# Modulation rows stored through a transpose, and two row tiles scaled at another place, in a one-layer diffusion backbone

## The chip, the cores and the metric

The kernel runs on one core of a Trainium2 chip. The metric is the device time of one execution in microseconds (us); below it is given as the median of three runs, and the profile comes from one further execution.

Names used here: PE is TensorE (matrix products), PEld its weight loads, ACT is ScalarE, DVE is VectorE, POOL is GpSimd, SP is SyncE, which issues most transfers (SPq in the profile). All work is float32. A product is made from three matmuls, since each operand is split into a high part and a low remainder: high by high, high by low, low by high.

## The reference

One layer, for 1024 latent tokens and 128 context tokens, width 1024. A conditioning vector gives six modulation vectors; the third (`ga1`) and the sixth (`ga2`) scale the two residual branches. The attention and Fourier part gives `merge_branches`, whose last product is with `w_out`. The rest, cut to what the change lies in:

```python
def modulation(cvec, w_ada, b_ada):
    m = jax.nn.silu(cvec) @ w_ada + b_ada
    return [t[:, None, :] for t in jnp.split(m, 6, axis=-1)]

def channel_mixer(h, w_ff1, w_ff2):
    return jnp.square(jax.nn.relu(h @ w_ff1)) @ w_ff2

def latent_layer(x, mod, ...):
    sh1, sc1, ga1, sh2, sc2, ga2 = mod
    ...
    x = x + ga1 * merge_branches(u_f, attn_o, g, w_fo, w_ao, w_out)
    h = rmsnorm(x, g2) * (1 + sc2) + sh2
    x = x + ga2 * channel_mixer(h, w_ff1, w_ff2)
    return x
```

The context tokens go through the same lines with the modulation of a learned constant vector. A last rmsnorm ends both.

## The kernel before, in words

**Phases.** Modulation and input projection; attention and Fourier mixing; the product with `w_ao`; the product with `w_out` with the first residual and norm; the first MLP weight (`ff1`) in sixteen passes of 256 columns; the second MLP weight; the last norm. The change lies from the end of the `w_ao` phase to pass 12 of ff1, and it takes some transfers out of the attention phase.

**What sets the order.** In the attention phase, and from the second group of the `w_out` phase to the first ff1 pass (`man`, a manual schedule), PE, DVE, ACT and POOL run in the order in which the code is written. Elsewhere, and for SP throughout, a scheduler of the framework sets the order of each engine from the code. Each engine works its list off in order. Buffers set waits: an instruction that overwrites a buffer waits for its last reader, a transfer included.

**w_out and first norm.** Nine tiles of 128 tokens (tile 8 is the context) stand in three groups; a product of one tile and half (`unit`, `major`, L1415 to L1417) collects in a PSUM bank. `fin_a` multiplies by `ga1`, adds the row of x (in `XS[t % 3]`, three row buffers which `row(t)`, L1559, loads), stores the result to `x1_d` (L1433) and squares it (L1434). `fin_b1` and `fin_b2` (L1444 to L1455) make the norm's factor `rs`. `fin_b3` (L1461) scales the row by it on ACT. `fin_c` transposes the scaled row by four 128x128 transposes on PE (L1473) for each half, and evicts them with scale and shift: the first half on ACT (L1478), the second on DVE (L1480). Tile 5 is scaled in place, in `XS[2]`; the others into buffers `ys`. The weight rows for group 2 come back split from `wo_d` (L1517); `load_wout` (L1520, cast L1521) loads them raw before.

**MLP operands.** From the transposed rows seven operands T[1] to T[7] are made (`t_hi`, a cast on ACT, L1363; `t_lo`, the remainder on DVE, L142), each with four column groups of tokens: the third tile pair, 6 and 7, is index 3. A pass of ff1 makes seven products `p1` to `p7` of such operands (`prod`, L1684 to L1686) in place of eight. In pass 0 they are made in parts (`part`): RA is the first three token groups, RB the last, which waits for tiles 6 and 7. `ev_part` (L1714) copies a finished part. `ff1_load` (L1379) loads two raw weights of a pass, which are split by L147 (cast on ACT) and L142; `ff1_sums` makes their sums (L1396 to L1399) and the operand `w4v` (cast L1402). `step_ctx` (L1740 to L1745) does the context's product with relu and square, `step_ctx2` (L1752) transposes it.

**Modulation rows.** `mods` holds the modulation vectors by column: partition p, block m, token kind `tok`. `ga_rows(k, row)` writes the eight blocks of vector k for both kinds as rows of `ga_d` in HBM, by eight POOL transfers (L1238) of 128 partitions by two elements of 4 bytes. `ga_put` (L1359) and others read such a row back for all partitions. It is called twice: `ga_rows(2, 0)` for `ga1`, ahead of the w_out phase, and `ga_rows(5, 2)` for `ga2` at the end of pass 12. A transfer leaves as soon as its blocks are there, so the first eight go out in the attention phase, and the second eight in four pairs between 1072.8 and 1232.4 us.

Of the kernel before, what the change touches and what calls it, by code (L numbers as in the profile page):

```python
# [14 lines left out]
ALU = mybir.AluOpType  # L15
# [3 lines left out]
P = 128  # L19
# [4 lines left out]
KC = D // P  # L24
# [32 lines left out]
def backbone_kernel(  # L57
# [27 lines left out]
    nc = tc.nc  # L85
    uid = [0]

    def nm(s):
        uid[0] += 1
        return f"{s}_{uid[0]}"  # L90
# [32 lines left out]
    def mmt():  # L123
        return pmm.tile([P, 512], F32, tag="mm", name=nm("mm"))
# [12 lines left out]
    ga_d = dp.tile([4, D], F32, name="ga_d")  # L137
# [3 lines left out]
    def sub(eng, dst, raw, hi):  # L141
        return eng.tensor_tensor(dst, raw, hi.bitcast(F32), ALU.subtract)  # L142
# [8 lines left out]
    def raw_w(shape):  # L151
        return wp.tile(shape, F32, tag="wraw", name=nm("wraw"), bufs=2)
# [6 lines left out]
    ident = const.tile([P, P], F32, name="ident")  # L159
# [7 lines left out]
    mods = const.tile([P, 48, 2], F32, name="mods")  # L167
# [3 lines left out]
    def mod(k, m, tok):  # L171
        return mods[:, k * 8 + m, tok : tok + 1]
# [39 lines left out]
    hs = list(zip(h_hi, h_lo))  # L212
# [57 lines left out]
    fold_bank = [mmt]  # L270
# [87 lines left out]
    with ExitStack() as sf:  # L358
        qa = sf.enter_context(tc.tile_pool(name="qa", bufs=6, space=PSUM))

        def bank6():
            return qa.tile([P, 512], F32, tag="x", name=nm("x"))
# [178 lines left out]
        for gi in range(4):  # L541
# [25 lines left out]
            px = bank6()  # L567
# [48 lines left out]
    with ExitStack() as s1x:  # L616
# [475 lines left out]
        for b, w in enumerate(blocks_):  # L1092
            if 0 in w[1]:
                continue
            k = KC * first[b]
# [134 lines left out]
    def gt():  # L1230
        return q3.tile([P, 512], F32, tag="x", name=nm("x"))

    fbank[0] = gt

    def ga_rows(k, row):
        for tok in range(2):
            for m in range(0, 8, 2):
                nc.gpsimd.dma_start(  # L1238
                    ga_d[row + tok, m * P : (m + 2) * P].rearrange("(m p) -> p m", p=P),
                    mods[:, k * 8 + m : k * 8 + m + 2, tok],  # L1240
                )

    def ga_load(pool, row, tag):
        out = []
# [78 lines left out]
    def tsel(n):  # L1323
        return (tev, TE[n]) if n in TE else (tbv, TB[n])
# [8 lines left out]
    def zh(i, n=1):  # L1333
        return ZR[:, i * HB : (i + n) * HB]

    ga1 = zh(0, 2)
    XS = [zh(11, 2), zh(13, 2), zh(15, 2)]
    SA = zh(13, 2)
    ys = {t: zh(5 + 2 * (t % 3), 2).rearrange("p (k c) -> p k c", k=KC) for t in range(NTT)}
# [21 lines left out]
    def t_hi(n, i, raw):  # L1361
        v, j = tsel(n)
        nc.scalar.copy(v[:, i, j, 0], raw)  # L1363

    def t_lo(n, i, raw):
        v, j = tsel(n)
        sub(nc.vector, v[:, i, j, 1], raw, v[:, i, j, 0])
# [7 lines left out]
    def ff1_load(p, order=(0, 1)):  # L1375
        raws[p] = [None, None]
        for kh in order:
            raw = raw_w([P, 4, 256])
            nc.sync.dma_start(  # L1379
                raw, w_ff1[kh * 512 : (kh + 1) * 512, p * 256 : (p + 1) * 256].rearrange("(k p) n -> p k n", p=P)  # L1380
            )
            raws[p][kh] = raw
# [66 lines left out]
    def fin_b2(t):  # L1449
        v, r, rs = rsd[t]  # L1450
        nc.vector.reciprocal(r, r)
        nc.vector.tensor_tensor(rs, r, r, ALU.mult)
        nc.vector.tensor_tensor(rs, rs, v, ALU.mult)
        nc.vector.tensor_scalar(rs, rs, -0.5, 1.5, ALU.mult, ALU.add)
        nc.vector.tensor_tensor(rs, rs, r, ALU.mult)  # L1455

    def fin_b3(t, n=1):
        rs = rsd.pop(t)[2]
        for i in range(n):
            hs = XS[(t + i) % 3] if t + i == 5 else ys[t + i].rearrange("p k c -> p (k c)")  # L1460
            nc.scalar.activation(hs, XS[(t + i) % 3], AF.Copy, scale=rs[:, i : i + 1])  # L1461

    def fin_b(t, n=1):
# [1 line left out]
        fin_b2(t)  # L1465
        fin_b3(t, n)

    def fin_c(t, kh):
        tok = 0 if t < 8 else 1
        px = mmt()  # L1470
        hn, yt = XS[t % 3] if t == 5 else ys[t].rearrange("p k c -> p (k c)"), ys[t]
        for q in range(4):
            nc.tensor.transpose(px[:, q * P : (q + 1) * P], hn[:, (kh * 4 + q) * P : (kh * 4 + q + 1) * P], ident)  # L1473
        for q in range(4):
            k = kh * 4 + q
            src = px[:, q * P : (q + 1) * P]
            if kh == 0:
                nc.scalar.activation(yt[:, k], src, AF.Identity, bias=mod(3, k, tok), scale=s2[:, k, tok : tok + 1])  # L1478
            else:
                nc.vector.tensor_scalar(yt[:, k], src, s2[:, k, tok : tok + 1], mod(3, k, tok), ALU.mult, ALU.add)  # L1480
# [47 lines left out]
    RA, RB, R4 = (0, 3), (3, 1), (0, 4)  # L1528
# [29 lines left out]
    def row(t):  # L1558
        nc.sync.dma_start(XS[t % 3], x_lat[t * P : (t + 1) * P, :] if t < 8 else x_ctx)  # L1559
# [7 lines left out]
    def major(gi, k):  # L1567
        for t in range(3 * gi, 3 * gi + 3):
            for h in range(2):
                wout_mm(b3[t, h], t, h, k, WO[k], WO_ORDER[gi])  # L1570
# [63 lines left out]
    fin_b2(5)  # L1634
    fin_b3(5)
    fin_c(4, 1)
    row(7)
    t_rest_m(1)
    r0, r1 = raws.pop(0)
    u1 = tuple(pz.tile([P, 4, 256], F32R, tag=tag, name=nm(tag), bufs=1) for tag in ("whi", "wlo"))  # L1640
# [2 lines left out]
    t_first(2)  # L1643
    fin_c(5, 0)
    fin_c(5, 1)
    row(8)
    major(2, 3)
    load_wout(2, 5)
    t_rest_m(2)
# [44 lines left out]
    def obuf(p, r, what):  # L1694
        return place[p][what][:, r[0] * P : (r[0] + r[1]) * P]
# [9 lines left out]
    def part(bank, n, r, new=False):  # L1705
        if new:
            st.setdefault((0, R4), {})[bank] = gt()
        prod(st[0, R4][bank], 0, n, r, cont=not new)

    def ev_part(r):  # L1710
        c = slice(r[0] * P, (r[0] + r[1]) * P)
        s_ = st[0, R4]
        s_["u2"] = obuf(0, R4, 0)
        nc.scalar.copy(s_["u2"][:, c], s_["a"][:, c])  # L1714
# [19 lines left out]
    def step_ctx(p):  # L1734
        ps = st[p, "ctx"] = mmt()
        (h0, l0), (h1, l1) = wu[p][1], wu[p][2]
        for k in range(KC):
            wh, wl = (h0, l0) if k < 4 else (h1, l1)
            wh, wl = wh[:, k % 4], wl[:, k % 4]
            nc.tensor.matmul(ps[:, :256], cth[:, k], wh, start=(k == 0), stop=False)  # L1740
            nc.tensor.matmul(ps[:, :256], cth[:, k], wl, start=False, stop=False)
            nc.tensor.matmul(ps[:, :256], ctl[:, k], wh, start=False, stop=(k == KC - 1))
        v = zh(4)[:, :256]
        nc.scalar.activation(v, ps[:, :256], AF.Relu)
        nc.scalar.activation(v, v, AF.Square)  # L1745
        st[p, "ctx"] = v
# [69 lines left out]
    y11, y12, y21, y22 = quarters(3)  # L1816
# [21 lines left out]
    ga_put(1)  # L1838
    part("a", 1, RA, True)
    fin_b2(7)  # L1840
    ev_part(RA)
    fin_c(6, 0)
    fin_c(6, 1)
    part("e", 4, RA, True)
    t_hi(1, 3, y11)
    fin_b3(7)
    t_lo(1, 3, y11)
    t_hi(2, 3, y21)
    t_lo(2, 3, y21)
    fin_c(7, 0)  # L1850
    fin_c(7, 1)
    nc.vector.tensor_tensor(y11, y12, y11, ALU.subtract)
    t6 = tmpt().rearrange("p (k c) -> p k c", k=4)
    nc.vector.tensor_tensor(t6, y22, y11, ALU.subtract)
    part("a", 1, RB)
    ev_part(RB)
    part("a", 2, RA)
    nc.scalar.copy(w4v[0], sb)
    sub(nc.vector, w4v[1], sb, w4v[0])
    wu[0]["u4"] = w4v  # L1860
    ff1_load(1)
    part("a", 2, RB)
    t_hi(6, 3, t6)
    t_lo(6, 3, t6)
    part("b", 6, RA, True)
    part("b", 6, RB)
    nc.vector.tensor_tensor(y12, y22, y12, ALU.subtract)
    t_hi(7, 3, y12)
    t_lo(7, 3, y12)
    t_hi(5, 3, y11)  # L1870
    step_p7(0)
    uh(1, 1)
# [312 lines left out]
    bank = None  # L2185
    for s, (j, p) in enumerate(steps):
# [13 lines left out]
        if p == 0:  # L2200
            if j != 3:
                bank = [gt() for _ in range(5 if j == 2 else 4)]
# [155 lines left out]
```

## Time and profile before

| | us |
|---|---|
| runs | 1656.18, 1657.26, 1659.58 |
| median | 1657.26 |
| the profiled execution | 1654.63 |
| its span, first to last instruction | 1652.9 |
| PE busy in it | 1610.2 |
| PE idle in it | 42.7 |

Of PE's idle time, 17.8 us lie in the first 100 us and 7.5 us in the last 53, both far from the change. In the list of waits a row names the engine and line that waited, what it waited for, the sum in us, how often and the longest. In a timeline a row has start, duration, engine and line, what is written from what, with shape; in brackets stands how long the engine was idle before, and what ended that.

### The profile page before, as it was taken

The numbers are of one execution on the slowest core, as the hardware profiler recorded it, in microseconds if no ns is written. First come the engines' busy times: TensorE is split into PE (matmuls) and PEld (weight loads), VectorE is DVE, ScalarE is ACT, GpSimd is POOL, SyncE is SP. The second block draws the span as 40 slices with busy tenths as digits, with TensorE's granted clock in tenths as the row PEclk, the third lists the DMA queues.
The fourth block names the chain that finished last, engine by engine and source line by source line (L and its number), as shares of the span: only waits on it lengthen the run. The fifth ranks groups of instructions, "written<-read, shape, count | busy, mean of one in ns | idle before, by whom it ended". The sixth has DMA issues, their size and how long they took to land.

```text
span 1652.9 us, 24756 instructions
## 1 busy us (share of the span) xinstructions
PE 1610.2 (97%) x8357; PEld 1412.5 (85%) x8357; DVE 1127.1 (68%) x2215; ACT 884.8 (54%) x1722; POOL 273.1 (17%) x399
## 2 busy tenths in 40 slices
PE   6999999999999999999999999999999999999998
PEld 5789889899889999889988888887888888888887
DVE  7644266867767865678658877766776588785764
ACT  7743455777677665564346564444445354444542
POOL 1020252555445332310000000000000200000000
PEclk9999999999999999999999999999999999999999
DMA  8342578556444333587575335445555995666841
GB/s 322 129 121 87 182 215 216 132 119 162 121 125 114 106 106 112 160 285 237 161 288 178 117 138 183 163 146 143 166 146 180 348 375 176 197 202 188 257 155 64
DMA packets 217351, 290.19 MB, mean 176 GB/s; under 512 B 27540, under 2 KB 142164, under 8 KB 217096
## 3 DMA queue, kind: packets, MB, share of 16 engines
q1 hardware_dynamic: 205768, 269.72, 52.6%
q0 software_dynamic: 11456, 18.90, 4.0%
q8 instruction: 66, 1.08, 0.3%
q14 instruction: 61, 0.50, 0.1%
HBM read 205.10 MB, written 83.44 MB: 175 GB/s over the span
## 4 chain that ended last, share of the span: by engine, by line
PE 74%; DVE 5%; DMA 3%; ACT 2%; issue 1%; SPq 0%; DVEq 0%; ACTq 0%
PE x L2083 6%; PE x L2085 6%; PE x L2084 6%; PE x L1684 5%; PE x L1686 5%; PE x L1685 5%; PE mm L195 4%; PE mm L197 4%; PE mm L196 4%; PE ptp L859 3%; PE x L197 2%; PE x L195 2%; PE x L196 2%; PE s L819 2%; PE s L820 2%; PE o L874 2%
## 5 line engine op out<-in xcount | busy, mean ns | idle before, releaser
L142 DVE TENSOR_TENSOR wlo<-wraw,whi 128x1024 fp32r<-128x1024 f32 x96 | 121.4, 1266 | 97.8 <-ACT whi L147 75.2
L833 ACT ACTIVATE pt<-pt,mx 128x513 f32<-128x513 f32 (+2 forms) x144 | 95.8, 666 | 82.9 <-DVE mx L821 64.5
L196 PE MATMUL mm<-BR,whi 128*128 128x384 f32 x408 | 137.1, 336 | 0.0
L2084 PE MATMUL x<-BR 128*128 128x512 f32 (+1 forms) x348 | 132.9, 382 | 0.0
L2085 PE MATMUL x<-BR 128*128 128x512 f32 (+1 forms) x348 | 132.5, 382 | 0.0
L2083 PE MATMUL x<-BR 128*128 128x512 f32 (+1 forms) x348 | 131.4, 382 | 0.0
L195 PE MATMUL mm<-BR,whi 128*128 128x384 f32 x360 | 128.1, 356 | 2.9 <-ACT z L717 1.6
L821 DVE CUSTOM_DVE_ANT_0 pt<-s,mask,nsink 128x512 f32<-128x512 f32 (+2 forms) x144 | 96.7, 673 | 40.4 <-PE s L820 38.2
L845 POOL TENSOR_SCALAR pt<-pt,mx 128x512 f32<-128x512 f32 (+2 forms) x144 | 94.8, 670 | 177.5 <-DVE mx L843 175.7
L197 PE MATMUL mm<-BR,wlo 128*128 128x384 f32 x360 | 121.6, 338 | 0.0
L147 ACT CAST whi<-wraw 128x1024 fp32r<-128x1024 f32 x62 | 64.9, 1049 | 100.1 <-DMA wraw<-in_w_ff_dram 53.7
L2056 ACT CAST BR<-aa 128x512 fp32r<-128x512 f32 x80 | 49.7, 621 | 105.5 <-PE x L2084 51.4
L142 DVE TENSOR_TENSOR pl<-ptp,ph 128x512 fp32r<-128x512 f32 x124 | 83.8, 687 | 23.1 <-ACT ph L862 21.7
L326 POOL TENSOR_TENSOR macc<-macc,mprod 128x512 f32<-128x512 f32 x70 | 93.7, 1338 | 7.7 <-ACT macc L324 2.5
L196 PEld LDWEIGHTS mm<-BR,whi 128*128 128x128 f32 x408 | 77.1, 189 | 6.0
L859 PE MATMUL ptp<-ident,pt 128*128 128x128 f32 x496 | 74.4, 274 | 4.0 <-DVE pl L142 3.9
L142 DVE TENSOR_TENSOR BR<-aa,BR 128x512 fp32r<-128x512 f32 x80 | 55.2, 690 | 33.2 <-ACT BR L2056 32.7
L862 ACT CAST ph<-ptp 128x512 fp32r<-128x512 f32 x124 | 70.5, 585 | 12.5 <-PE ptp L859 11.2
L195 PE MATMUL mm<-BT,whi 128*128 128x384 f32 x216 | 76.8, 356 | 0.0
L2084 PEld LDWEIGHTS x<-BR 128*128 128x128 f32 x348 | 65.4, 188 | 12.9
L2083 PEld LDWEIGHTS x<-BR 128*128 128x128 f32 x348 | 65.4, 188 | 12.9
L2085 PEld LDWEIGHTS x<-BR 128*128 128x128 f32 x348 | 65.4, 188 | 12.6
(470 smaller groups left out, 4792.8 us busy)
## 6 DMA issues: line engine op xcount, KB each, us to landing
aa<-hr_d SPq DMA_DIRECT2D x108, 256.0 KB
ab<-in_w_ff_dram SPq DMA_DIRECT2D x108, 256.0 KB
hr_d<-ZR SPq DMA_DIRECT2D x104, 256.0 KB
wraw<-in_w_in_dram SPq DMA_DIRECT2D x41, 512.0 KB
wraw<-in_w_ff_dram SPq DMA_DIRECT2D x34, 512.0 KB
mraw<-in_w_ada_dram SPq DMA_DIRECT2D x96, 128.0 KB
z_d<-z SPq DMA_DIRECT2D x48, 192.0 KB
q_d<-qt SPq DMA_DIRECT2D x48, 192.0 KB
```

The costliest lines, as they stand in the source:

```text
L142: return eng.tensor_tensor(dst, raw, hi.bitcast(F32), ALU.subtract)
L195: nc.tensor.matmul(out, ah, bh, start=start, stop=False)
L196: nc.tensor.matmul(out, ah, bl, start=False, stop=False)
L197: return nc.tensor.matmul(out, al, bh, start=False, stop=stop).ins
L326: nc.gpsimd.tensor_tensor(acc, acc, pr_, ALU.add)
L821: nc.vector.tensor_tensor_reduce(out=pt[:, e, :n], in0=sp[:, :n], in1=mask[:, m0 : m0 + n], scale=-0.125, scalar=nsink[:, h0 + e : h0 + e ...
L833: nc.scalar.activation(pt[:, e, : n + 1], pt[:, e, : n + 1], AF.Exp, bias=mx[:, e : e + 1], scale=-1.0, accum_out=mx[:, 2 + e : 3 + e],)
L845: ins = nc.gpsimd.tensor_scalar(pt[:, e, :n], pt[:, e, :n], mx[:, 4 + e : 5 + e], 1.0, ALU.mult, ALU.mult)
L859: nc.tensor.transpose(pst[:, h * P : (h + 1) * P], u["pts"][h // 2][:, h % 2, b * P : (b + 1) * P], ident)
L2083: nc.tensor.matmul(ps, xh, bh, start=start, stop=False, skip_group_check=cont)
L2084: nc.tensor.matmul(ps, xh, bl, start=False, stop=False, skip_group_check=cont)
L2085: nc.tensor.matmul(ps, xl, bh, start=False, stop=stop, skip_group_check=cont)
```

## The change

It has four parts.

1. `ga_rows` no longer stores columns. PE transposes the 128x8 block of each token kind into a PSUM bank as rows, ACT copies 8x256 elements to `zh(3)`, and one SP transfer writes the rows, in pieces of 128 elements (512 bytes). The 16 POOL transfers go away.
2. Tile 5 is scaled into `XS[1]`, and `fin_c(5, ...)` reads it there. The loads of rows 7 and 8 change places, since row 8 uses `XS[2]` and row 7 `XS[1]`.
3. Tile 7 is scaled straight behind its factor. Its first transposes take their bank from `gt` (the pool of product banks) instead of `mmt`. Behind it `part("a", 2, RA)` comes ahead of `part("a", 1, RB)`, the operands 6 and 7 of the last group ahead of the split of `w4v`, and `part("b", 6, RA)` ahead of `part("a", 2, RB)`.
4. In `step_ctx` the eight matmuls with the low part of the context stand behind the sixteen with its high part.

```diff
     def ga_rows(k, row):
+        pr = fold_bank[0]()
         for tok in range(2):
-            for m in range(0, 8, 2):
-                nc.gpsimd.dma_start(
-                    ga_d[row + tok, m * P : (m + 2) * P].rearrange("(m p) -> p m", p=P),
-                    mods[:, k * 8 + m : k * 8 + m + 2, tok],
-                )
+            nc.tensor.transpose(pr[:8, tok * P : (tok + 1) * P], mods[:, k * 8 : k * 8 + 8, tok], ident)
+        rows = zh(3)[:8, : 2 * P]
+        nc.scalar.copy(rows, pr[:8, : 2 * P])
+        nc.sync.dma_start(
+            ga_d[row : row + 2].rearrange("t (m p) -> m t p", p=P), rows.rearrange("m (t p) -> m t p", t=2)
+        )
...
-            hs = XS[(t + i) % 3] if t + i == 5 else ys[t + i].rearrange("p k c -> p (k c)")
+            hs = XS[1] if t + i == 5 else ys[t + i].rearrange("p k c -> p (k c)")
...
-    def fin_c(t, kh):
+    def fin_c(t, kh, bank=mmt):
         tok = 0 if t < 8 else 1
-        px = mmt()
-        hn, yt = XS[t % 3] if t == 5 else ys[t].rearrange("p k c -> p (k c)"), ys[t]
+        px = bank()
+        hn, yt = XS[1] if t == 5 else ys[t].rearrange("p k c -> p (k c)"), ys[t]
...
     fin_c(4, 1)
-    row(7)
+    row(8)
...
     fin_c(5, 1)
-    row(8)
+    row(7)
...
             nc.tensor.matmul(ps[:, :256], cth[:, k], wl, start=False, stop=False)
+        for k in range(KC):
+            wh = (h0 if k < 4 else h1)[:, k % 4]
             nc.tensor.matmul(ps[:, :256], ctl[:, k], wh, start=False, stop=(k == KC - 1))
...
     fin_b2(7)
+    fin_b3(7)
     ev_part(RA)
     fin_c(6, 0)
     fin_c(6, 1)
     part("e", 4, RA, True)
     t_hi(1, 3, y11)
-    fin_b3(7)
     t_lo(1, 3, y11)
     t_hi(2, 3, y21)
     t_lo(2, 3, y21)
-    fin_c(7, 0)
+    fin_c(7, 0, gt)
     fin_c(7, 1)
     nc.vector.tensor_tensor(y11, y12, y11, ALU.subtract)
     t6 = tmpt().rearrange("p (k c) -> p k c", k=4)
     nc.vector.tensor_tensor(t6, y22, y11, ALU.subtract)
+    part("a", 2, RA)
     part("a", 1, RB)
+    nc.vector.tensor_tensor(y12, y22, y12, ALU.subtract)
     ev_part(RB)
-    part("a", 2, RA)
+    t_hi(6, 3, t6)
+    t_lo(6, 3, t6)
+    t_hi(7, 3, y12)
+    t_lo(7, 3, y12)
     nc.scalar.copy(w4v[0], sb)
     sub(nc.vector, w4v[1], sb, w4v[0])
     wu[0]["u4"] = w4v
     ff1_load(1)
+    part("b", 6, RA, True)
     part("a", 2, RB)
-    t_hi(6, 3, t6)
-    t_lo(6, 3, t6)
-    part("b", 6, RA, True)
     part("b", 6, RB)
-    nc.vector.tensor_tensor(y12, y22, y12, ALU.subtract)
-    t_hi(7, 3, y12)
-    t_lo(7, 3, y12)
```

In the changed kernel a line number is 2 higher from `ga_rows` on and 4 higher behind `step_ctx`. The first place is ACT round the scaling of tile 7. Before, from the root of tile 7's factor (L1446) on; L1714 copies part "a", the first L1478 evicts tile 6, L1363 is `t_hi`, L1858 the cast of `w4v`:

```order
L1446 ACTIVATE rsw_10107<-rsw_10107 128x1
L1714 COPY ZR<-x_10121 128x384
L1478 ACTIVATE ZR<-mm_10140,mods,s_95 128x128 x4
L1363 CAST BR<-ZR 128x512
L1461 ACTIVATE ZR<-ZR,rsw_10107 128x1024
L1363 CAST BR<-ZR 128x512
L1478 ACTIVATE ZR<-mm_10176,mods,s_95 128x128 x4
L1714 COPY ZR<-x_10121 128x128
L1858 CAST BT<-wraw_9835 128x1024
```

Now:

```order
L1448 ACTIVATE rsw_10104<-rsw_10104 128x1
L1463 ACTIVATE ZR<-ZR,rsw_10104 128x1024
L1716 COPY ZR<-x_10118 128x384
L1480 ACTIVATE ZR<-mm_10138,mods,s_95 128x128 x4
L1365 CAST BR<-ZR 128x512 x2
L1480 ACTIVATE ZR<-x_10173,mods,s_95 128x128 x4
L1716 COPY ZR<-x_10118 128x128
L1365 CAST ER<-ZR 128x512 x2
L1867 CAST BT<-wraw_9832 128x1024
```

The scaling has moved ahead of the copy, the eviction of tile 6 and the first cast; two more casts now stand ahead of the cast of `w4v` (L1858, now L1867).

The second place is SP at the beginning of the w_out phase. Before:

```order
L1520 DMA wraw_9329<-in_w_out_dram 128x1024
L1520 DMA wraw_9353<-in_w_out_dram 128x1024
L1359 DMA ZR<-ga_d 128x1024
L1559 DMA ZR<-in_x_lat_dram 128x1024 x3
L1520 DMA wraw_9377<-in_w_out_dram 128x1024
```

Now:

```order
L1522 DMA wraw_9326<-in_w_out_dram 128x1024
L1522 DMA wraw_9350<-in_w_out_dram 128x1024
L1561 DMA ZR<-in_x_lat_dram 128x1024
L1241 DMA ga_d<-ZR 8x2x128
L1561 DMA ZR<-in_x_lat_dram 128x1024 x2
L1361 DMA ZR<-ga_d 128x1024
L1522 DMA wraw_9374<-in_w_out_dram 128x1024
```

The store L1241 is new in this queue, and the load `ga_put` (L1361), which reads what it writes, stands three transfers behind it in place of the POOL stores of long before, with the remaining w_out loads behind it.

The third place is PE at the end of the first context product. Before, the last three matmuls of it, then product 6 of pass 1 (`ER` is the operand):

```order
L1740 MATMUL mm_10426<-BT 128x256
L1741 MATMUL mm_10426<-BT 128x256
L1742 MATMUL mm_10426<-BT 128x256
L1684 MATMUL x_10506<-ER,whi_10469 128x512
L1685 MATMUL x_10506<-ER,whi_10469 128x512
L1686 MATMUL x_10506<-ER,wlo_10470 128x512
```

Now:

```order
L1742 MATMUL mm_10423<-BT 128x256
L1743 MATMUL mm_10423<-BT 128x256
L1746 MATMUL mm_10423<-whi_9897,BT 128x256 x4
L1746 MATMUL mm_10423<-BT 128x256 x4
L1686 MATMUL x_10503<-ER,whi_10466 128x512
L1687 MATMUL x_10503<-ER,whi_10466 128x512
L1756 MATMUL mm_10450<-ident,ZR 128x128 x2
L1742 MATMUL mm_10476<-whi_10280,BT 128x256
```

The two transposes of the context result (L1756, before L1752 and 22 matmuls behind the product) now stand two matmuls behind it, and the next context product follows at once, ahead of the product with the low part of the weight.

## The prediction

> **What bounds the kernel now.** I read the page first, for the engine that sets the end, then the idle time of that engine by stretch, then its waits, and only then the timeline round each wait.
>
> ```profile
> PE 1610.2 (97%) x8357; PEld 1412.5 (85%) x8357; DVE 1127.1 (68%) x2215; ACT 884.8 (54%) x1722; POOL 273.1 (17%) x399
> ```
>
> PE (TensorE) is busy 1610.2 of 1652.9 us, and no other engine is near that. The change takes no product away, so it can gain only what PE stands idle, 42.7 us, or runs at a lower clock. Where that lies, in stretches (columns: stretch and length, busy time of PE, PEld, DVE, ACT and POOL, granted clock, DMA share, GB/s):
>
> ```profile
> 860.00:960.00 100.00, 97.81 (x499) 83.00 (x499) 79.95 (x172) 62.98 (x125) 0.00 (x0) 1.00 0.46 152
> 1200.00:1600.00 400.00, 400.00 (x1824) 333.35 (x1823) 288.50 (x468) 182.21 (x318) 11.45 (x18) 1.00 0.70 225
> ...
> PE x L1684 <- ACT BT L1402: 2.7, 1, 2.7
> PE mm L1473 <- ACT ZR L1461: 1.8, 2, 1.0
> ...
> PE x L1686 <- DVE wlo L142: 0.4, 1, 0.4
> PE x L1684 <- ACT ZR L1714: 0.4, 1, 0.4
> ```
>
> From 860 us on, where almost all of the change lies, PE idles 2.19 us up to 960 and nothing in 1200 to 1600. The waits of PE (who waits for whom: us in total, times, longest) explain the former and give the rest: 1.8 + 0.4 before 960 (L1473 twice, L1684), 0.4 soon after (L1686), 2.7 later. That is 5.3 us in five waits, and the change touches the neighbourhood of each. More than these it cannot save there.
>
> **Tile 5: 1.1 us saved.**
>
> ```profile
> 896.32 1.51 ACT L1478 ACTIVATE ZR<-mm,mods,s 128x128 f32<-128x128 f32 x4
> 900.51 1.15 ACT L1461 ACTIVATE ZR<-ZR,rsw 128x1024 f32<-128x1024 f32 x1 [2.69 <-DMA x_d<-ZR]
> ...
> 895.19 0.44 SPq L1433 DMA_DIRECT2D x_d<-ZR  x1
> 900.55 0.32 SPq L1517 DMA_DIRECT2D wlo<-wo_d  x1
> ...
> 895.39 0.39 PE L1417 MATMUL x<-whi,BT 128*128 128x512 f32 x1
> 895.62 1.03 PE L1473 MATMUL mm<-ident,ZR 128*128 128x128 f32 x8
> ...
> 901.71 1.09 PE L1473 MATMUL mm<-ident,ZR 128*128 128x128 f32 x8 [0.96 <-ACT ZR L1461]
> ...
> 897.19 0.16 DVE L1455 TENSOR_TENSOR rsw<-rsw 128x1 f32<-128x1 f32 x1
> ```
>
> ScalarE scales tile 5 in place, so L1461 must wait until the store of the row's second half (issued 895.19) has read it: 2.69 us idle. Its factor was ready at 897.35 and ScalarE free at 897.83. Into another buffer it can start there and end near 899.0, long before PE asks for it. PE's idle of 0.96 is counted from the drawn end of the product ahead, and that is drawn too long: the one at 895.39 lasts 0.39, but the transposes of the tile before follow it after 895.62 − 895.39 = 0.23. So each wait costs 0.16 more than its idle, and here **1.12** is saved: PE can start the transposes at 900.6.
>
> The two loads change places on SP. That of row 8 now needs the old buffer, so it waits for the same store, to about 900.5, and the wo_d loads stand behind it. They were issued at 900.55, so they slip by one issue, 0.4 us. Between 0 and 0.4 us of cost; since PE's idle up to 960 holds no wait for them, I take 0.
>
> **Tile 7: 1.5 us saved.**
>
> ```profile
> 929.51 0.16 DVE L1455 TENSOR_TENSOR rsw<-rsw 128x1 f32<-128x1 f32 x1
> ...
> 929.73 0.48 ACT L1714 COPY ZR<-x 128x384 f32<-128x384 f32 x1 [1.02 <-PE x L1686]
> 930.23 1.51 ACT L1478 ACTIVATE ZR<-mm,mods,s 128x128 f32<-128x128 f32 x4
> 931.76 0.62 ACT L1363 CAST BR<-ZR 128x512 fp32r<-128x512 f32 x1
> 932.29 1.14 ACT L1461 ACTIVATE ZR<-ZR,rsw 128x1024 f32<-128x1024 f32 x1
> ...
> 933.49 1.09 PE L1473 MATMUL mm<-ident,ZR 128*128 128x128 f32 x8 [0.83 <-ACT ZR L1461]
> ...
> 936.23 0.45 PE L1684 MATMUL x<-BR,BT 128*128 128x384 f32 x1 [0.36 <-ACT ZR L1714]
> ...
> 928.24 10.78 SPq L1379 DMA_DIRECT2D wraw<-in_w_ff_dram  x2
> ```
>
> The factor is there at 929.67, but L1461 stands behind three other instructions and ends at 933.43. Ahead of them it runs from 929.7 to 930.9. Queued behind it are the copy L1714 (now to 931.3), four evictions (to 932.8) and the first two casts (to 934.0). Who needs them: the third waiting product, which adds to the bank that L1714 copies, stands behind tile 7's transposes in the new order, so at 933.3 or later, 2 us clear of the copy. Both waits go: 0.83 + 0.16, **1.0**, and 0.36 + 0.16, **0.52**. What is late next: the second of the two weight loads of pass 1 (out at 938.7, the end of the 10.78 less its own 0.4) waits for a subtraction that now stands behind two more casts and two subtractions of 128x512; at 0.62 each, by the cast at 931.76, that is up to 2.5 us, and the work that is ahead of it is 1.5 us earlier. So it slips by up to 1.0 us. Its first use lies in the next pass, so the cost is between 0 and 1.0; I take 0.
>
> **The small stores: 4.5 us saved.**
>
> ```profile
> 1135.80 1.42 POOL L1238 DMA_DIRECT2D ga_d<-mods  x2 [61.56 <-DVE mods L282]
> DMA to landing us min/median/max: 9.0/9.7/10.2
> ...
> 1126.58 0.38 SPq L1379 DMA_DIRECT2D wraw<-in_w_ff_dram  x1
> 1140.65 0.38 SPq L1379 DMA_DIRECT2D wraw<-in_w_ff_dram  x1
> ...
> 1130.68 1.05 ACT L147 CAST whi<-wraw 128x1024 fp32r<-128x1024 f32 x1 [3.76 <-DMA wraw<-in_w_ff_dram]
> 1149.86 1.04 ACT L147 CAST whi<-wraw 128x1024 fp32r<-128x1024 f32 x1 [6.63 <-DMA wraw<-in_w_ff_dram]
> ...
> 1152.43 0.51 PE L1684 MATMUL x<-ER,BT 128*128 128x512 f32 x1 [2.67 <-ACT BT L1402]
> 1153.07 0.63 PE L1684 MATMUL x<-ER,whi 128*128 128x512 f32 x1
> 1156.64 0.40 PE L1684 MATMUL x<-ER,whi 128*128 128x512 f32 x1
> ...
> 1140.00:1146.00 6.00, 6.00 (x32) 5.10 (x31) 1.61 (x4) 2.07 (x4) 0.00 (x0) 1.00 1.03 99
> ```
>
> Of a pair of L1238 stores, each of 256 elements of 4 bytes, the first goes out at 1135.80; such stores take 9.0 to 10.2 us to land. The weight load issued at 1126.58 arrives 4.1 us later; the one of 1140.65 only at 1149.86, 9.2 us later, while the DMA engines count as fully busy (1.03) and move 99 GB/s. ScalarE takes its work in order, so the cast L1402 behind that one runs late and PE stands for 2.67 + 0.16 = 2.83. Then the clock is down: the 11 steps from 1152.43 to 1156.64 take 4.21 us where 11 × 0.23 is 2.53, so 1.7. Together **4.55**. Without the element stores the load should land in 4 to 5 us and the cast run by 1147. The four pairs of stores in the attention cost PE nothing that I find; their rows go without gain.
>
> The rule for the price of such a stall is weighed here. The Trainium skill (TensorE: Matmul & The Clock Gate, Part 1) has the clock halved after about 3.4 us of an idle window. By that the 2.67 us of idle need not have cost any clock, a new stall of this kind would cost 2.83 alone, and the first rival below would come to 1653.4. The trace differs: behind this shorter stall the 11 steps average 0.38 us instead of 0.23, so the row decides.
>
> **Added: 0.5 us.** Four transposes on PE. The trace has none of this shape; the nearest is the x8 at 933.49, 1.09 us long with its last end drawn 0.16 too long: 0.93, 0.12 each. At most 0.28 each, the drawn length of a context matmul of twice the width (964.62, below); at least nothing, if they fall where PE waits. Bounds 0 to 1.1 for four; I take 0.45, by the nearest row. Two ScalarE copies of 8x256 (nearest 0.37, below) fall into idle ScalarE time and cost nothing, or 0.4 each without it. The store goes out on SP, and the first one is new work in a queue: ga_put must wait until it has landed, and behind it stand five w_out loads.
>
> ```profile
> 830.90 15.20 SPq L1520 DMA_DIRECT2D wraw<-in_w_out_dram  x5
> ...
> 843.44 1.05 ACT L1521 CAST whi<-wraw 128x1024 fp32r<-128x1024 f32 x1 [4.10 <-DMA wraw<-in_w_out_dram]
> 846.89 1.07 PE L1415 MATMUL x<-whi,BR 128*128 128x512 f32 x4
> ```
>
> The copy can run at about 825.9 and the store go at 826.5. Tile 5's store above takes 5.3 us (895.19 to 900.51); that puts ga_put at 832 and the loads 1 us late. The last cast ends at 844.49, PE asks for it at 846.89: 2.4 us of cover. With 9.7 us, as the element stores have, it would be 836 and the cover gone (third rival). I take 5.3, since these are rows of many bytes, and 0.
>
> **The context products: nothing.**
>
> ```profile
> 964.62 0.28 PE L1742 MATMUL mm<-BT 128*128 128x256 f32 x1
> ...
> 965.77 0.50 PE L1686 MATMUL x<-ER,wlo 128*128 128x512 f32 x1 [0.40 <-DVE wlo L142]
> ...
> 964.94 0.38 ACT L1744 ACTIVATE ZR<-mm 128x256 f32<-128x256 f32 x1
> 966.15 0.42 ACT L1745 ACTIVATE ZR<-ZR 128x256 f32<-128x256 f32 x1
> ```
>
> The wait of 0.40 + 0.16 goes, 0.56, since 24 context products now stand ahead of the low part. But the two context transposes now come two products behind the first context, 0.6 us after its last matmul starts, and need relu and square: 0.32 to the start, 0.38 and 0.42, some 1.1 with both. A new wait of 0.4 to 0.7; I take 0.6. Net 0, from 0.2 gain to 0.15 loss.
>
> **Sum.** 1.12 + 1.0 + 0.52 + 4.55 + 0.56 − 0.6 − 0.45 = 6.7 us off the profiled execution of 1654.63 (span 1652.9 and 1.7 round it): 1647.9. That execution is 2.63 under the median of the three runs, 1657.26, so the time by the same measure is **1650.6 us**, 0.4% less. A measurement of this kernel tells about 0.2%, 3.3 us, from no change.
>
> **Rivals.**
>
> *One stall comes back.* From the w_out phase on, the order of SP is made anew, and of all engines in the passes after the hand-written part. Before, one of fifteen casts L1402 came late; a new lateness at one place costs what this one did, 2.83 to 4.55: 1653.4 to 1655.2. For: on SP, the store of the rows in pass 12 now stands ahead of a weight load. Against: 400 us without a wait from 1200 on.
>
> *The late load had another cause.* The element stores go, and the load at 1140 is late as before: 4.55 kept, 1655.2. For: stores also left at 1072.8, 1189.3 and 1231.7 without a stall on PE. Against: 5 us of busy DMA at a low rate just then. Here the Trainium skill (DMA: Bandwidth & Descriptors, Specifications) gives 512 bytes as the least transfer at line rate, with a read-modify-write below; by it the stall goes. The landing times of 9.0 to 10.2 us agree with slow small stores, though no row shows the cause.
>
> *ga_put blocks the w_out loads.* Landing takes 9.7 instead of 5.3: ga_put goes at 836.2, and the loads come 5.3 us late against 2.4 of cover: 2.9 of wait and 1.7 for the clock behind it, 4.6: 1655.2. For: the waiting transfer now stands in the loads' own queue. Against: rows of many bytes.
>
> *Slower.* The re-made loop has late casts L1402 in several passes: the weight loads on SP, which go out in a new order among the stores, land after their use. Each costs 4.55 by the stall at 1152. The gain of 6.7 is gone at one and a half of them; three give 13.65 − 6.7 = 7.0 over, 1664.3. For: ScalarE in order gives one late load to PE at once. Against: only one in the whole loop before, and with the element stores the largest disturbance of these loads is gone.
>
> **Chances.** Forecast 0.62; one stall back 0.12; other cause 0.08; ga_put 0.06; slower by late casts 0.12. A stall back at its low price still is faster by over 0.2%, 0.04 of its share. Faster 0.66, same 0.22, slower 0.12. The range: below, the transposes and the new context wait at nothing, 1649.5, and 2 us for the median of the runs, which lay 1.1 and 2.3 from the ends of theirs; above, the cases at 1655.2 with as much: 1647.5 to 1657.5. What is left out is above all the slower case.
>
> **What would show it.** Tile 5: L1463 ends before PE's last product, no wait of PE's transposes for it. Tile 7: the same, and no wait for the copy. Stores: no POOL instruction behind 1000 us but those of the weights, every wraw load in 4 to 6 us, clock 1.00 in 1146 to 1200. Context: a wait of PE's transposes L1756 of about half a us. Wrong it would be by a PE wait in 830 to 850 for a w_out cast, or any PE wait over 1 us in 960 to 1600.

## The result, and the profile after

The changed kernel took 1651.77 us (median of 7 runs) beside 1656.6 for the kernel before (7 runs in all), 4.8 us less: the ratio is 0.9963, with a 95% interval of 0.9946 to 0.9979, so it is faster by 0.2 to 0.5%. The profiled execution took 1648.85 us, its span is 1647.1.

The page of the profile after:

```profile
PE 1609.0 (98%) x8361; PEld 1411.4 (86%) x8361; DVE 1127.6 (68%) x2215; ACT 886.7 (54%) x1724; POOL 262.1 (16%) x383
```

Three stretches of it (columns as before):

```profile
860.00:960.00 100.00, 99.80 (x511) 85.19 (x510) 81.61 (x178) 64.21 (x126) 0.00 (x0) 1.00 0.46 156
1140.00:1200.00 60.00, 60.00 (x299) 50.71 (x298) 42.35 (x71) 28.59 (x45) 0.00 (x0) 1.00 0.48 164
1200.00:1600.00 400.00, 400.00 (x1827) 333.19 (x1826) 287.69 (x470) 183.95 (x325) 10.03 (x16) 1.00 0.69 227
```

PE's idle time in 860 to 960 fell from 2.19 to 0.20 us, that in 1146 to 1200 is gone, and 1200 to 1600 is as full as it was. Two small waits are new there (from PE's list of waits):

```profile
PE x L1686 <- ACT whi L147: 0.3, 1, 0.3
PE x L1417 <- DMA whi<-wo_d: 0.2, 1, 0.2
```

To see where the time went, one PE instruction of each stage is taken in both timelines, and the starts are subtracted. The table has start before, start after, difference, and the gain of the stage, which is the difference less the one above:

| PE instruction | before | after | difference | stage |
|---|---|---|---|---|
| first w_out product | 822.29 | 823.16 | +0.87 | |
| transposes of tile 4 | 895.62 | 896.45 | +0.83 | −0.04 |
| of tile 5 | 901.71 | 901.43 | −0.28 | −1.11 |
| of tile 6 | 929.53 | 929.42 | −0.11 | +0.17 |
| of tile 7 | 933.49 | 932.37 | −1.12 | −1.01 |
| of tile 8 | 955.54 | 953.78 | −1.76 | −0.64 |
| a context transpose in the loop | 1132.79 | 1131.39 | −1.40 | +0.36 |
| a later one | 1182.12 | 1176.17 | −5.95 | −4.55 |
| last matmul | 1645.26 | 1639.61 | −5.65 | +0.30 |

Of the +0.87 ahead of w_out, 0.13 are two of the new transposes; the rest comes from the start of the kernel (PE's first L422 at 11.51 and 12.23 us). This offset was anywhere from −3.5 to +1.6 us in the kernels below, which hardly differ there, so stages are compared without it: from the first w_out product on the change took off 6.5 us.

How tile 5, tile 7, the row store and the late cast look in the timelines after, ACT first:

```profile
827.46 0.36 ACT L1240 COPY ZR<-mm 8x256 f32<-8x256 f32 x1 [1.27 <-DVE BT L142]
...
898.54 1.16 ACT L1463 ACTIVATE ZR<-ZR,rsw 128x1024 f32<-128x1024 f32 x1
...
929.30 1.15 ACT L1463 ACTIVATE ZR<-ZR,rsw 128x1024 f32<-128x1024 f32 x1 [1.06 <-DVE rsw L1457]
930.36 0.46 ACT L1716 COPY ZR<-x 128x384 f32<-128x384 f32 x1
...
1144.81 1.06 ACT L1404 CAST BT<-wraw 128x1024 fp32r<-128x1024 f32 x1 [2.09 <-PE x L1687]
1145.77 1.04 ACT L147 CAST whi<-wraw 128x1024 fp32r<-128x1024 f32 x1
```

PE and SP:

```profile
823.03 0.38 PE L1238 MATMUL mm<-ident,mods 128*8 128x128 f32 x2
901.43 1.03 PE L1475 MATMUL mm<-ident,ZR 128*128 128x128 f32 x8
932.37 0.60 PE L1475 MATMUL x<-ident,ZR 128*128 128x128 f32 x4
963.42 0.50 PE L1686 MATMUL x<-ER,whi 128*128 128x512 f32 x1 [0.28 <-ACT whi L147]
964.15 0.44 PE L1756 MATMUL mm<-ident,ZR 128*128 128x128 f32 x2
...
827.85 0.31 SPq L1241 DMA_DIRECT2D ga_d<-ZR  x1
831.42 0.33 SPq L1361 DMA_DIRECT2D ZR<-ga_d  x1
```

Tile 5's scaling starts at 898.54 without a wait for the store, and PE's transposes come without an idle bracket. Tile 7's scaling starts at once behind its factor. `ga_put` goes 3.6 us behind the row store, with no wait of PE for the w_out casts. One thing the reader should note for below: the cast of w4v (L1404) now stands *ahead* of L147 on ACT, where it stood behind it before. So two things could have removed the wait at 1152: the stores, or this order.

### The profile page after: what moved, and what is told of

The parts are those of the page before. It is cut to its first block, busy times and chain, and to the rows that moved or that the text cites. A ratio compares the mean times of both kernels' runs of the same rounds, so it can differ in the third digit from the quotient of the medians.

```text
span 1647.1 us, 24717 instructions
## 1 busy us (share of the span) xinstructions
PE 1609.0 (98%) x8361; PEld 1411.4 (86%) x8361; DVE 1127.6 (68%) x2215; ACT 886.7 (54%) x1724; POOL 262.1 (16%) x383
## 4 chain that ended last, share of the span: by engine, by line
PE 80%; DVE 3%; DMA 1%; ACT 1%; issue 1%; SPq 0%; DVEq 0%; ACTq 0%
PE x L1686 6%; PE x L1687 6%; PE x L1688 6%; PE x L2087 6%; PE x L2089 6%; PE x L2088 6%; PE mm L195 4%; PE mm L197 4%; PE mm L196 4%; PE ptp L859 3%; PE x L197 2%; PE x L195 2%; PE x L196 2%; PE x L1417 2%; PE x L1419 2%; PE x L1418 2%
## 5 line engine op out<-in xcount | busy, mean ns | idle before, releaser
L147 ACT CAST whi<-wraw 128x1024 fp32r<-128x1024 f32 x62 | 64.9, 1048 | 88.1 <-DMA wraw<-in_w_ff_dram 39.9
```

## The experiments

Every kernel was compared with the kernel before on its own chip. For each the stages are given as in the table above.

### One part alone, and one part undone

**Row storage alone.** The kernel before with only this edit:

```diff
     def ga_rows(k, row):
+        pr = fold_bank[0]()
         for tok in range(2):
-            for m in range(0, 8, 2):
-                nc.gpsimd.dma_start(...)
+            nc.tensor.transpose(pr[:8, tok * P : (tok + 1) * P], mods[:, k * 8 : k * 8 + 8, tok], ident)
+        rows = zh(3)[:8, : 2 * P]
+        nc.scalar.copy(rows, pr[:8, : 2 * P])
+        nc.sync.dma_start(...)
```

> The kernel before with the first part of the change alone (modulation rows turned on TensorE and stored as 512-byte pieces). Theory (the 4-byte stores made one weight load late): the wait of TensorE for the cast of w4v at 1152 (2.67 us, 4.5 with the clock) is gone, every raw ff weight lands in under 6 us, 4.2 us less in all (4.5 less 0.3 for transposes): 0.26% faster. Rival (the late load had another cause, and the new order of the other parts removed it): the wait of about 2.7 us is still there and the time within 1 us of before.

Ratio 0.9964 (0.9952 to 0.9976). Its timeline, SP and ACT:

```profile
1137.08 0.38 SPq L1381 DMA_DIRECT2D wraw<-in_w_ff_dram  x1
...
1141.61 1.05 ACT L147 CAST whi<-wraw 128x1024 fp32r<-128x1024 f32 x1 [1.72 <-DMA wraw<-in_w_ff_dram]
...
1143.09 1.04 ACT L1404 CAST BT<-wraw 128x1024 fp32r<-128x1024 f32 x1
```

ACT has the order of before, L147 ahead of the cast of w4v, but the load lands 4.5 us after its issue instead of 9.2. The stage with the wait at 1152 gives −4.60 us, and PE idles nowhere in 1100 to 1200. The new order is not needed to remove the wait.

**Row storage undone.** The changed kernel with `ga_rows` as before, the other three parts kept.

> The changed kernel with the modulation rows stored as before (16 GpSimd stores of 256 elements of 4 bytes); the other three parts kept. Theory of the 4-byte stores: weight loads issued within about 9 us of such a store land 9 to 10 us after issue; if one of them is cast ahead of w4v, TensorE waits again, 1 to 3 us with clock loss behind it, and the time is 2.7 us under before (tiles 5 and 7) instead of 5.8. Rival (new order of the loop removed the wait): no wait over 1 us of TensorE in the loop, the time 5.5 to 6 us under before.

Ratio 1.0018 (1.0005 to 1.0031): slower than before, so neither the theory's time (2.7 us under before) nor the rival's (5.5 to 6) came out. **The context order alone**, the stores as before:

> The kernel before with the fourth part alone (low-part matmuls of the context behind the others). Forecast: within 0.2 us of before at the first context product (one wait of 0.4 traded for another of 0.3 to 0.6). Theory of the 4-byte stores: the stores still leave one by one, so late loads of 9 us are still there, and where one is cast ahead of w4v TensorE waits 1 to 3 us. Rival (order of the loop): the wait at 1152 vanishes although the stores are there.

One run, 1657.7 us, where the kernel before had a median of 1652.06 on this chip. The forecast for the first context product held (the stage around it moved by 0.19 us). In both the wait at 1152 is gone (−4.58 in its stage), and both lose more at another place. The timeline of the kernel with the context order alone, SP, ACT and PE:

```profile
1227.82 0.38 SPq L1379 DMA_DIRECT2D wraw<-in_w_ff_dram  x1
1236.35 0.38 SPq L1379 DMA_DIRECT2D wraw<-in_w_ff_dram  x1
...
1242.63 1.05 ACT L147 CAST whi<-wraw 128x1024 fp32r<-128x1024 f32 x1 [5.39 <-DMA wraw<-in_w_ff_dram]
1248.61 1.04 ACT L147 CAST whi<-wraw 128x1024 fp32r<-128x1024 f32 x1 [4.20 <-DMA wraw<-in_w_ff_dram]
...
1250.62 0.79 PE L1686 MATMUL x<-BR,wlo 128*128 128x512 f32 x1 [5.15 <-DVE wlo L142]
```

The last pair of stores left at 1227.32 and 1228.02. Two loads come late one behind the other: the one issued at 1227.82 is cast 14.8 us later, the one of 1236.35 12.3 us later, and PE waits 5.15 us for the low part split from the second. Its stage loses 7.13 us; in the kernel with the row storage undone 6.16 are lost in the same way. So both theories held one half: the new order does move the cast out of the way of the late load at 1140, and as long as the 4-byte stores are there PE runs into those of 1227 and 1236.

**The same stores, later.** The kernel before, with the second eight stores reading a copy made at the end of pass 12, so that they all leave from 1227.2 to 1232.9:

```diff
     def ga_rows(k, row):
+        src = mods[:, k * 8 : k * 8 + 8, :]
+        if k == 5:
+            v = zh(3)[:, :16].rearrange("p (m t) -> p m t", t=2)
+            nc.vector.tensor_copy(v, src)
+            src = v
...
-                    mods[:, k * 8 + m : k * 8 + m + 2, tok],
+                    src[:, m : m + 2, tok],
```

> The kernel before, with the second eight 4-byte stores reading from a copy of the rows' block that VectorE makes at the end of pass 12, so that all eight go out together at about 1233 us and none at 1073, 1136 or 1189. Theory: no wait of 2.7 us at 1152, 4 us less up to 1200; the loads in flight behind 1233 land late (9 us or more), at a cost between 0 and 4.5 us there. Rival (another cause): the wait at 1152 is as before.

Ratio 0.9993 (0.9984 to 1.0002). On ACT and PE:

```profile
1143.93 1.05 ACT L147 CAST whi<-wraw 128x1024 fp32r<-128x1024 f32 x1 [1.37 <-DMA wraw<-in_w_ff_dram]
1246.58 1.05 ACT L147 CAST whi<-wraw 128x1024 fp32r<-128x1024 f32 x1 [8.84 <-DMA wraw<-in_w_ff_dram]
...
1249.06 0.50 PE L1691 MATMUL x<-BR,wlo 128*128 128x512 f32 x1 [0.65 <-DVE wlo L142]
```

The late load moved with the stores. The wait at 1152 went (−4.59), the load issued at 1234.70 landed at 1246.58, 11.9 us later, and 3.24 us were lost there.

### Small pieces or the queue

**The old stores on SP** (`nc.sync` for `nc.gpsimd` in the old `ga_rows`):

> The kernel before with the sixteen stores of 4-byte elements issued by SyncE instead of GpSimd. Theory (the pieces): raw ff weight loads near them still land 9 us or more after issue, since the same engines carry the same small pieces; a wait of TensorE of 2 to 5 us stays somewhere in the loop. Rival (the queue): none, and 4 us less than before from 1100 on. SyncE also works in order here, so a load behind such a store in its list may be issued later; that shows as a late issue, not as a late landing.

Ratio 0.9991 (0.9981 to 1.0002). SP, ACT and PE:

```profile
1132.12 0.88 SPq L1238 DMA_DIRECT2D ga_d<-mods  x2
1137.23 0.38 SPq L1379 DMA_DIRECT2D wraw<-in_w_ff_dram  x1
...
1146.22 1.04 ACT L147 CAST whi<-wraw 128x1024 fp32r<-128x1024 f32 x1 [6.58 <-PE x L1686]
...
1148.79 0.50 PE L1684 MATMUL x<-ER,BT 128*128 128x512 f32 x1 [2.62 <-ACT BT L1402]
```

The bracket at 1146.22 names PE, which had long been done: the load issued at 1137.23 is what came last, 9.0 us after. The wait is that of before (2.62 and 2.67), and its stage moved by 0.04 us. The queue of issue does not matter.

**The new store on GpSimd** (`nc.gpsimd` for `nc.sync` in the new `ga_rows`):

> The changed kernel with the row store issued by GpSimd instead of SyncE: pieces of 512 bytes, but in the queue of before. Theory (the 4-byte pieces are what delays the loads): as the changed kernel within 1 us, no late load. Rival (the GpSimd queue is what delays): a raw ff weight load landing 9 us or more after issue behind 1229, and a wait of TensorE of 1 to 5 us at 1235 to 1255.

Ratio 0.9969 (0.9958 to 0.9980). No late load in the loop (−4.58), against the rival. The landing times of its two stores, from the view of their line:

```profile
DMA to landing us min/median/max: 2.2/3.9/5.6
```

What happened in the w_out phase (SP, ACT, PE):

```profile
831.30 0.42 SPq L1361 DMA_DIRECT2D ZR<-ga_d  x1
836.58 9.52 SPq L1522 DMA_DIRECT2D wraw<-in_w_out_dram  x3
...
843.44 1.04 ACT L1523 CAST whi<-wraw 128x1024 fp32r<-128x1024 f32 x1 [4.84 <-DMA wraw<-in_w_out_dram]
...
844.54 0.50 PE L1417 MATMUL x<-whi,BR 128*128 128x512 f32 x1 [2.46 <-ACT whi L1523]
```

The stores land in 2.2 and 5.6 us, where those of 4-byte pieces took 9.0 to 10.2 in the kernel before. But this kernel loses 4.1 us in the w_out phase, which was not expected: PE waits for the cast of the load issued at 836.58. It is the wait which the prediction's third rival named, but it did not come by that rival's way: `ga_put` did not hold the load back. Counted from the first w_out product (818.92 here) the load went out after 17.7 us; the same load of the changed kernel, at 840.50, went out after 17.3. But here it took 6.8 us to land, where it took 4.5 in the changed kernel and in the kernel before. One difference can be seen: `ga_put`, issued at 831.30, was in flight until 838.7, while in the changed kernel it had landed at 836.8, before that load went out. That this slowed the load was not tried.

For all of these kernels, the loads of ff weights for which ACT or DVE waited between 1000 and 1270 us, with the time from the load's issue to the start of the waiting instruction:

| kernel | stores | longest, us |
|---|---|---|
| before | 4-byte, GpSimd | 10.3, 9.2 |
| context order alone | 4-byte, GpSimd | 14.8, 12.3 |
| row storage undone | 4-byte, GpSimd | 14.6, 11.3 |
| tile 5 alone (below) | 4-byte, GpSimd | 9.9, 8.8 |
| the same stores, later | 4-byte, GpSimd | 11.9 |
| the old stores on SP | 4-byte, SP | 9.9, 9.6 |
| row storage alone | 512 bytes, SP | 5.4 |
| the new store on GpSimd | 512 bytes, GpSimd | 5.8 |
| changed | 512 bytes, SP | 5.2 |

At the end of pass 12 the kernels with 512-byte pieces issue one store in place of eight, and the next load goes out 5 to 6 us behind it. That distance is not what spares the load: in the context order alone the load of 1236.35 went out 8.3 us behind the last pair of 4-byte stores and was late. Nor is it the amount: that pair carries 2 KB, the one store 8 KB. The size of the pieces was not varied apart from their number.

### Tile 5 and the loads behind it

**Tile 5 alone:**

> The kernel before with the second part alone (tile 5 scaled into a free buffer, the loads of rows 7 and 8 exchanged). Forecast: 1.1 us less at tile 5's transposes. Given back behind it by the wo_d loads that slip: 0.1 to 0.2 us as in the changed kernel, or up to 3.5 us as in the kernel with the old stores (2.0 us of wait at the w_out weights, and the clock). The wait at 1152 stays (4.5 us with the clock), if the loop's order is that of before.

Ratio 0.9999 (0.9987 to 1.0010). The tile's stage gave −1.12, the next one +3.76, for this wait of PE:

```profile
918.16 0.50 PE L1415 MATMUL x<-whi,BT 128*128 128x512 f32 x1 [2.21 <-DMA whi<-wo_d]
...
1155.34 0.50 PE L1684 MATMUL x<-ER,BT 128*128 128x512 f32 x1 [1.54 <-ACT BT L1402]
```

The wait at 1152, expected to stay at 4.5 us, shrank: it is at 1155.34 here, 1.54 us long, since its load was cast 8.8 us after issue. In 1153 to 1160 the granted clock was 1.00, and the wait cost 1.8 us in all (its stage gave −2.72 of 4.55).

**The changed kernel a second time**, for another profile:

> The changed kernel once more, on the chip of the next three, for a second profile and a time beside theirs. Expected: 0.35 to 0.45% under before; by the stages: tile 5 about 1.1 us less, tiles 7 and 8 about 1.6 less, the 1152 wait gone (4.4 less). Open after the row-storage kernel alone gave 0.36%: whether tiles 5 and 7 add their 2.5 us to it (then about 0.5% here) or not.

Ratio 0.9966 (0.9956 to 0.9976). The stages are those of the first profile within 0.25 us, but for one: from tile 5 to tile 6 it lost 3.57 us instead of 0.17. Its SP and PE:

```profile
898.09 0.33 SPq L1561 DMA_DIRECT2D ZR<-in_x_ctx_dram  x1
899.39 0.32 SPq L1519 DMA_DIRECT2D wlo<-wo_d  x1
899.87 0.32 SPq L1519 DMA_DIRECT2D whi<-wo_d  x1
900.49 0.33 SPq L1561 DMA_DIRECT2D ZR<-in_x_lat_dram  x1
908.81 0.42 SPq L1519 DMA_DIRECT2D whi<-wo_d  x1
...
915.43 0.50 PE L1417 MATMUL x<-whi,BT 128*128 128x512 f32 x1 [2.03 <-DMA whi<-wo_d]
```

The stretch behind the wait:

```profile
916.00:920.00 4.00, 4.00 (x12) 3.10 (x12) 1.88 (x3) 0.46 (x1) 0.00 (x0) 0.60 0.01 4
```

Both row loads now go out among the wo_d loads, four transfers of 512 KB within 2.4 us. The last wo_d load, issued at 908.81, takes 6.6 us to the waiting product, and the clock granted behind the wait is 0.60. From its issue to the weight load of PE that uses it, that last load took 4.3 to 4.5 us where row 7's load went out ahead of the wo_d loads (before, row storage alone, the context order alone, tile 5's part undone) and 4.8 (twice), 5.2, 6.5, 6.6 and 6.8 us where both row loads stood among them.

**Tile 5's part undone**, the other three kept:

> The changed kernel without its second part: tile 5 scaled in place, the loads of rows 7 and 8 in their old order. Theory (the exchanged row loads run into the wo_d loads, which have no slack): TensorE waits 0.3 to 1.0 us for tile 5's scaling as before, but not for the last wo_d load (under 0.1 us of idle, against 2.0 in the second profile of the changed kernel); from tile 5 to tile 6 the shift against before stays within 0.2 us where the changed kernel lost 0.2 to 3.6. In all 6 us under before, 0 to 2.5 us under the changed kernel. Rival (the wo_d wait comes from the other parts): it is still there, the time 1 us over the changed kernel.

Ratio 0.9974 (0.9964 to 0.9983). PE's list of waits has what was expected, and no wait for wo_d:

```profile
PE mm L1475 <- ACT ZR L1463: 1.0, 1, 1.0
```

**The row loads held back.** Tile 5 scaled into the free buffer, but the loads of rows 7 and 8 behind the last wo_d load. Two writes of one column, which the loads overwrite, make them wait:

```diff
     fin_c(4, 1)
-    row(8)
...
     fin_c(5, 1)
-    row(7)
...
+    nc.vector.memset(XS[1][:, 0:1], 0.0)
+    row(7)
     sub(nc.vector, u1[1], r0, u1[0])
...
     unit(8, 0)
+    nc.vector.memset(XS[2][:, 0:1], 0.0)
+    row(8)
     fin_b1(7)
```

> The changed kernel with the loads of rows 7 and 8 held back behind the last wo_d load (two VectorE writes of one column into their buffers make them wait). Theory: neither the wait for tile 5's scaling nor the one for wo_d; 1.1 us less than before at tile 5 and kept up to tile 6; 6.5 to 7 us under before, the fastest of all. Rival (the wo_d loads themselves are slow, whatever lies beside them): the wait of 0.2 to 2 us at the w_out weights stays. Risk: row 7 lands later than its sum on VectorE, which would show as a wait of tile 7.

Ratio 0.9968 (0.9957 to 0.9980). SP and the weight load of PE:

```profile
907.82 0.38 SPq L1519 DMA_DIRECT2D whi<-wo_d  x1
910.05 0.33 SPq L1561 DMA_DIRECT2D ZR<-in_x_lat_dram  x1
...
912.37 0.19 PEld L1417 LDWEIGHTS x<-whi,BT 128*128 128x128 f32 x1 [0.43 <-DMA whi<-wo_d]
```

The last wo_d load takes 4.55 us again, and PE itself does not idle for it. Tile 5's stage gave −1.12 and the next one −0.04: the gain is kept. By the medians the kernel is 6.4 us under before, close to what was expected. **The same with the context order of before:**

> As the one before, with the context matmuls in their old order (fourth part undone). The stages showed 0.2 to 0.35 us lost in the loop with the new order and none with the old: 0.1 to 0.4 us less than with it, not to be told apart by the time. Rival: the old order brings back a wait over 1 us in the loop.

Ratio 0.9969 (0.9956 to 0.9981); the loop gave 0.5 us more. On the chip of these three, **the changed kernel once more**:

> The changed kernel again, beside the three others on the same chip. Theory of the wo_d loads: its runs lie in two groups some 3.5 us apart, as the wait for the last wo_d load is short (0.2 us idle) or long (2.0 us and the clock); the profile shows one of the two. Median 5 to 6 us under before.

Ratio 0.9974 (0.9964 to 0.9984), with the short wait for wo_d (0.2 us). Its eleven runs, from 1645.55 to 1650.85 us, do not fall into two clear groups, so that part of the expectation did not come out.

The gains by stage in us; "w4v" is the stage with the wait at 1152, "loop" the rest from the first context product to the last matmul. The last column also holds the way to tile 4 (−0.27 to +0.32 us, with the new store on GpSimd +4.11):

| kernel | tile 5 | to tile 6 | tiles 7, 8 | w4v | loop | all from w_out |
|---|---|---|---|---|---|---|
| changed, first profile | −1.11 | +0.17 | −1.65 | −4.55 | +0.66 | −6.5 |
| changed, second | −1.11 | +3.57 | −1.64 | −4.58 | +0.46 | −3.6 |
| changed, third | −1.11 | +0.19 | −1.65 | −4.55 | +0.66 | −6.7 |
| row storage alone | −0.64 | −0.08 | −0.03 | −4.60 | +0.21 | −5.4 |
| tile 5 alone | −1.12 | +3.76 | 0.00 | −2.72 | +0.01 | −0.1 |
| tile 5's part undone | +0.03 | −0.25 | −1.64 | −4.55 | +0.66 | −5.4 |
| row loads held back | −1.12 | −0.04 | −1.64 | −4.55 | +0.66 | −7.0 |
| the same, old context order | −1.11 | −0.01 | −1.64 | −4.59 | +0.20 | −7.3 |
| row storage undone | −1.12 | +3.51 | −1.64 | −4.58 | +6.77 | +2.9 |
| context order alone | +0.13 | −0.09 | −0.02 | −4.58 | +7.72 | +2.9 |
| the same stores, later | +0.11 | +0.11 | −0.01 | −4.59 | +3.24 | −0.8 |
| the old stores on SP | +0.15 | 0.00 | −0.03 | −0.04 | 0.00 | −0.2 |
| the new store on GpSimd | −1.11 | +0.59 | −1.65 | −4.58 | +0.46 | −2.2 |

The −0.64 of the row storage alone is at the unchanged tile 5: the store that it waits for landed earlier in that execution. By these stages the kernel with the row loads held back and the old context order is the best, 0.6 to 0.8 us under the better profiles of the changed kernel; by the times it cannot be told from it (0.9969 and 0.9974, with intervals 0.002 wide). Nor can the row storage alone (0.9964) be told by the times from the whole change (0.9963, 0.9966 and 0.9974): what the other three parts add is seen in the stages only.

## Why the prediction came out

The forecast was 6.7 us off and 1650.6 us. Measured were 1651.77 us, a ratio of 0.9963 (4.8 us between the medians), and in the profile 6.5 us from the first w_out product on. That the profile came so near is partly luck: its execution had the short wait for the last wo_d load, while the second profile of the same kernel, with the long one, gave 3.6 us.

- **Tile 5, 1.12:** measured 1.11 in each profile of the changed kernel. What the exchange of the row loads costs was bounded by 0 to 0.4 and taken as 0; it measured 0.17, 0.19 and 3.57. This is the step that failed: it counted the delay of one issue on SP, and took PE's idle, which held no wait for wo_d, as proof of slack. There was none, as the weight load of PE already waited 0.39 us for the last of them in the kernel before (the line below). And the cost was not the issue but a second row load of 512 KB in flight among the wo_d loads, where there had been one. Holding both back removes it (shown in two profiles, −0.04 and −0.01). Why the load takes 4.8 us in one execution and 6.6 in another of the same kernel is open.

```profile
915.72 0.19 PEld L1415 LDWEIGHTS x<-whi,BT 128*128 128x128 f32 x1 [0.39 <-DMA whi<-wo_d]
```

- **Tile 7, 1.0 and 0.52:** measured 1.0 and 0.64. The second weight load of pass 1 went out 0.9 us later against the first w_out product, as bounded, and in the kernel with the row loads held back and the old context order no wait of PE follows from it.
- **The small stores, 4.55:** measured 4.55 to 4.60. The cause holds: with stores of 4-byte pieces at least one ff weight load took over 9 us in every kernel, with 512-byte pieces none over 5.8, whichever queue issued them, and the late load followed the stores when these were moved. Not foreseen was that the new loop order would by itself have moved the wait to a worse place (7.1 us).
- **Transposes, 0.45:** the two at 823.03 take 0.13 up to the next product at 823.16, where the estimate had 0.23 for a pair. In the row storage alone 0.21 are lost behind pass 12, where the other pair stands.
- **The context order, 0:** at the first context product the trade came out as said in size: waits of 0.28 + 0.16 and, by the step from 963.75 to 964.15 instead of 0.23, 0.17, for 0.56 before. But the first of them was for L147, not for the transposes. Over the whole loop the part costs 0.5 us (+0.66 against +0.20 in the two kernels that differ in it alone). No wait of PE shows in those passes; where the rest is lost is open.
- **The first rival** (a stall comes back) did not happen in the loop. **That the late load had another cause** is refuted by the row storage alone. **The third rival** did not happen in the changed kernel (the store let `ga_put` go after 3.6 us, 5.3 were assumed), but PE did wait there, 2.46 us, with the store on GpSimd, for a load that took 6.8 us and was not held back. **The slower case**, late loads behind a re-made order, is what the changed kernel would have been without its first part: 1.0018, with one stall of 6.2 us and one of 3.5.

The clock's price held: behind 2.03 us of idle the granted clock was 0.60 and 1.4 us more were lost. The Trainium skill (TensorE: Matmul & The Clock Gate, Part 1) puts the fall of the clock behind some 3.4 us of an idle window; here it fell behind 2.0 and 2.7, and not behind 1.54.

## What to carry to other kernels

A store in 4-byte pieces can cost far from where it is issued: look for loads that take twice as long as their like, and for what left in the microseconds ahead of them. When a change moves a large load, it is not enough that no engine waits for the loads beside it now; look whether their readers already run at the edge, on PE's weight loads too. When parts are changed together, subtract the starts of the same instruction stage by stage: it resolves some 0.1 us, where the eleven times of the third run of the changed kernel spread over 5.

## What was not expected of the hardware

A pair of stores of 1 KB each, in 4-byte pieces, delayed 512 KB loads by 3 to 10 us, from either queue: the late ones in the table were cast 8.8 to 14.8 us after their issue, where no load took over 5.8 with 512-byte pieces. Eight such stores in one go delayed one load, no more than a single pair did (11.9). Not every pair does it: in the kernel before, the two loads round the pair of 1072.8 landed after 4.9 us each, and the one behind the pair of 1231.7 after 5.9. What decides it is open. The Trainium skill (DMA: Bandwidth & Descriptors, Specifications) says that pieces under 512 bytes are read, modified and written; that they also hold up other transfers by this much is what the runs show, and through which part of the DMA engines is open.
